# A two-layer decoder trunk: the last layer serves its expert groups in numerical order

## The chip, the cores and the metric

The kernel runs on one core of one Trainium2 chip. The core has a TensorE (PE in the profile; its weight loads are listed apart as PEld), a VectorE (DVE), a ScalarE (ACT), a GpSimd (POOL) and a SyncE (SP). Here SP does little but issue the DMAs that bring the weights from HBM into on-chip memory; 16 DMA engines move them. The metric is the device time of one execution in microseconds (us), and a kernel's time is the median over its runs.

## What is computed

There are 256 tokens of width 1024 and two layers. Each layer has a token mixer of four attention kinds, a cross-attention into 256 memory tokens, and a mixture of experts. The change is in the last of these. Cut down, it is:

```python
g_idx = jnp.argmax(xs @ w_group + b_group, axis=-1)            # one of 8 groups for each token
e_logits = (xs @ w_expert + b_expert).reshape(s, 8, 4)[jnp.arange(s), g_idx]
top_val, top_idx = lax.top_k(e_logits, 2)                      # two of the group's 4 experts
top_w = jax.nn.softmax(top_val, axis=-1) * g_weight
gates = one_hot(g_idx[:, None] * 4 + top_idx, 32) . top_w
hid = jax.nn.silu(xs @ w_gate[e]) * (xs @ w_up[e])             # for each expert e, 1024 -> 256
ff = sum over e of (hid * gates[:, e]) @ w_down[e]             # 256 -> 1024
x = layer_norm(ALPHA * x + ff)
```

An expert has three weight matrices (gate, up, down), each 1 MB as the kernel loads it. A layer has 8 groups of 4 experts, so 96 such loads. How many tokens an expert has depends on the data.

## The kernel before

**A group's work.** `moe` runs over the groups in the order of the table `SERVED` (line 34), one call of `expert(g)` for each (lines 1404 to 1476). The four experts of a group are worked on side by side: each has 32 columns of the 128-wide tiles. One pass therefore takes up to 32 tokens of each expert. A group's first pass is: the gate product (`up_to`, L1277, 64 matmuls) and its silu (L1281, on ACT), the up product (again L1277) and the multiplication with the silu (L1284, on DVE), a gather of the next group's tokens by matmuls with a 0/1 matrix (L1227, with L460 and L462 behind it), two transposes of the hidden values (L1290), and the down product (`rows`, L1306, with L1310 and L1311 behind it), whose results go back to the tokens' places (`back`, L1322 and L1327).

**Further passes.** Where an expert has more than 32 tokens, `over` (L1368) takes branches for a second pass, beyond 64 for a third, and so on. They stand between the first pass's transposes and its down product. In a group that isn't in `SPREAD` each further pass is a `whole` one: gather, gate, up, down. In a group that is (group 0 of the last layer), the further passes first do only gather, gate and up (`part`), each keeping its hidden values in a tile of its own; then the gate and up weights are given back (`free(g, 0, 8)`), and only then come these passes' down products (`rest`), and the group's own.

**The weights' places.** All weights of a layer stand in one list, the plan, in the order in which they will be used; for the experts the plan follows `SERVED` too (line 233): for each group 4 gate, 4 up and 4 down matrices. In the last layer's expert stage the loads go into 21 slots of 1 MB: 6 named main, 7 named ext that belong to this stage, 2 more ext and the two halves of M, and R, VM, KT and xx, which the attention has no more use for. `feed` (L255 to L280) issues the plan's next load on SP as soon as a slot is free, and SP takes them strictly in that order. `free` and `done` give a slot back: the 8 of a group's gate and up matrices after the last pass that uses them, that is behind the branches of `over`, and the 4 of its down matrices after its own down product. SP takes part in the branches, so a load behind `over` waits until TensorE has come through them.

**Known and unknown counts.** The first 21 expert loads are issued (at L270) before the router has run, for every expert. Later ones are issued at L275 inside a branch (L274) on the expert's token count, and are left out where it is 0.

**Hints.** `foresee` places a branch hint for TensorE ahead of a branch. `TELL` says at which of the eight steps of the up product the one for a group's second pass stands: in the last layer after step 3, and for the group that is served first after all eight, since its count is read only then. The group that is served first also does `prepare` (L1243 to L1255) between its gate and up products. `FIRST` and `GNUM` follow from `SERVED`: they say which number a group has in the code by which tokens are found.

Of the kernel before, what the change touches and what calls it, by code (L numbers as in the profile page):

```python
# [30 lines left out]
KEYS = 4  # L31


SERVED = [(0, 1, 2, 3, 4, 5, 6, 7), (1, 3, 0, 2, 4, 5, 6, 7)]
SPREAD = [(), (0,)]
TELL = [(3, 6), (3, 8)]


FIRST = [o[0] for o in SERVED]
GNUM = [[f if g == 0 else 0 if g == f else g for g in range(8)] for f in FIRST]  # L40
# [130 lines left out]
def trunk(ctx, tc, a, out, dbg=None, depth=DEPTH):  # L171
# [10 lines left out]
    def one(pool, name, shape, dt=F32):  # L182
        return tiles(pool, name, 1, shape, dt)[0]
# [27 lines left out]
    def square(l, m, q):  # L211
        wsq_i[l][m][q] = item(a["wsq"][l, m, q])
# [11 lines left out]
    for l in range(depth):  # L224
# [5 lines left out]
        for m in (3, 4):  # L230
            for q in range(4):
                square(l, m, q)
        for g, h in [(g, h) for g in SERVED[l + 1 == depth] for h in range(3)]:
            ids = exp_i[l].setdefault(g, {})
# [859 lines left out]
    def moe(l, pz, pb):  # L1094
# [3 lines left out]
        ff = one(pz, "ff", [128, 2, D])  # L1098
        served, spread = SERVED[late], SPREAD[late]
        follow = dict(zip(served, served[1:]))  # L1100
# [507 lines left out]
```

## Time and profile before

| What | Value |
|---|---|
| Time, median of 3 runs | 1009.5 us (1008.58 to 1012.58) |
| The profiled execution's own time | 1013.67 us |
| Its span, first to last instruction | 1011.9 us |
| TensorE matmul busy | 923.1 us, 91% |
| VectorE busy | 503.3 us, 50% |
| ScalarE busy | 340.9 us, 34% |
| Bytes moved by the DMAs | 272.59 MB, mean 269 GB/s |
| Stretch from 757 us to the end: DMA share, GB/s | 0.73, 295 |

The profile is of one execution. A row of the timeline gives start, duration, engine, line, operation and operands of one instruction or of several that are merged; in square brackets stands how long the engine was idle before it and what ended that. A row of the windows gives, for a stretch of time, each engine's busy us and instruction count, then TensorE's granted clock, the mean busy share of the 16 DMA engines, and what they moved in GB/s. Rows of the waits give a waiting line and what it waited for, then the sum in us, the number of waits and the longest.

The last layer's expert stage begins at about 757 us. Its groups were served in the order 1, 3, 0, 2, 4, 5, 6, 7. Group 0 took three further passes, group 2 one, the others none.

### The profile page before, as it was taken

To read this page: it belongs to the slowest core of one execution; us is meant where nothing else is said; L and a number is where in the kernel's file an instruction comes from. 1 tells how busy PE (TensorE), PEld (TensorE's weight loads), DVE (VectorE), ACT (ScalarE), POOL (GpSimd) and SP (SyncE) were. 2 spreads that over 40 slices of the span, in tenths; PEclk is the share of its full clock that TensorE was granted. 3 is DMA by queue.
4 is the path that set the end of the run, shared out by engine and by line. 5 is a ranking of instruction groups with operands and counts; after the bars stand their busy time and mean duration, and the time that the engine had idled before them with its cause. 6 is when DMAs were issued, how large, how long until landed. Compare 5 with 4: busy or idle time off the path is not lost. (4 is left out here: it accounts for less than half of the span.)

```text
span 1011.9 us, 19936 instructions
## 1 busy us (share of the span) xinstructions
PE 923.1 (91%) x7948; PEld 688.2 (68%) x7948; DVE 503.3 (50%) x1258; ACT 340.9 (34%) x736; POOL 0.2 (0%) x4
## 2 busy tenths in 40 slices
PE   7899999999998688989899999999999888997885
PEld 7888987898754354856368899789885564444541
DVE  5755755544653333323466575554465414644434
ACT  5454855343411121011144475435442121121111
POOL 0000000000000000000000000000000000000000
PEclk9999999999999899999999999999999999999998
DMA  9842334538769988999786244553784994719995
GB/s 351 343 147 99 134 128 161 209 125 331 293 268 422 424 348 367 424 425 420 250 336 229 108 147 180 174 208 110 288 351 196 421 387 183 318 58 421 422 363 203
DMA packets 43774, 272.59 MB, mean 269 GB/s; under 512 B 4832, under 2 KB 5344, under 8 KB 13280
## 3 DMA queue, kind: packets, MB, share of 16 engines
q1 hardware_dynamic: 43472, 270.26, 68.2%
q8 instruction: 86, 1.41, 0.5%
q14 instruction: 72, 0.59, 0.2%
q10 hardware_dynamic: 144, 0.33, 0.1%
HBM read 269.52 MB, written 1.05 MB: 267 GB/s over the span
## 5 line engine op out<-in xcount | busy, mean ns | idle before, releaser
L432 DVE SCALAR_TENSOR_TENSOR wl<-main,wh 128x1024 fp32r<-128x1024 f32 (+1 forms) x93 | 112.2, 1211 | 112.1 <-ACT wh L431 111.9
L431 ACT ACTIVATE wh<-main 128x1024 fp32r<-128x1024 f32 (+1 forms) x93 | 97.3, 1052 | 116.5 <-PE bank L438 68.3
L437 PE MATMUL bank<-xh,wh 128*128 128x256 f32 x368 | 108.8, 298 | 5.6 <-ACT xh L488 3.6
L438 PE MATMUL bank<-xl,wh 128*128 128x256 f32 x368 | 105.8, 288 | 1.0 <-DVE xl L432 0.6
L439 PE MATMUL bank<-xh,wl 128*128 128x256 f32 x368 | 104.9, 286 | 0.0
L1277 PE MATMUL bank<-ext,xg 128*32 128x256 f32 x912 | 88.2, 392 | 2.9 <-DMA ext<-exp 2.8
L1327 DVE TENSOR_TENSOR ff<-ff,bank 128x512 f32<-128x512 f32 x84 | 53.2, 681 | 49.9 <-PE bank L1322 49.9
L437 PEld LDWEIGHTS bank<-xh,wh 128*128 128x128 f32 x368 | 71.1, 194 | 7.0 <-ACT xh L488 4.1
L438 PEld LDWEIGHTS bank<-xl,wh 128*128 128x128 f32 x368 | 71.3, 194 | 2.2 <-DVE xl L432 0.9
L439 PEld LDWEIGHTS bank<-xh,wl 128*128 128x128 f32 x368 | 71.4, 194 | 0.1
L1277 PE MATMUL bank<-main,xg 128*32 128x256 f32 x640 | 66.1, 384 | 2.4 <-DMA main<-exp 2.4
L460 ACT ACTIVATE xg<-bank,prmb 128x128 f32<-128x128 f32 x64 | 24.0, 456 | 123.3 <-PE bank L1227 117.2
L1310 ACT ACTIVATE y<-bank,sm 128x512 fp32r<-128x512 f32 (+1 forms) x46 | 30.7, 669 | 103.5 <-PE bank L1306 76.1
L1322 PE MATMUL bank<-y,dt 128*128 128x512 f32 (+1 forms) x184 | 56.9, 422 | 7.9 <-DVE y L1311 7.2
L1306 PE MATMUL bank<-ext,dn 128*32 128x512 f32 (+1 forms) x212 | 46.6, 670 | 17.5 <-PEq L1368 6.8
L437 PE MATMUL bank<-wh,oh 128*128 128x512 f32 (+1 forms) x160 | 60.9, 380 | 0.0
L439 PE MATMUL bank<-wh,ol 128*128 128x512 f32 (+1 forms) x160 | 59.1, 369 | 0.0
L1322 PEld LDWEIGHTS bank<-y,dt 128*128 128x128 f32 x184 | 29.6, 188 | 43.2 <-ACT y L1310 16.4
L438 PE MATMUL bank<-wl,oh 128*128 128x512 f32 (+1 forms) x160 | 59.0, 369 | 0.0
L1277 PEld LDWEIGHTS bank<-ext,xg 128*32 128x32 f32 x912 | 42.6, 112 | 22.5 <-issue 4.7
L1227 PEld LDWEIGHTS bank<-dn,xhat 128*128 128x128 f32 x448 | 51.1, 192 | 5.8 <-issue 4.9
L1227 PE MATMUL bank<-dn,xhat 128*128 128x128 f32 x448 | 53.7, 278 | 0.0
(300 smaller groups left out, 2008.7 us busy)
## 6 DMA issues: line engine op xcount, KB each, us to landing
ext<-exp SPq DMA_DIRECT2D x75, 1024.0 KB, 16.6
main<-exp SPq DMA_DIRECT2D x54, 1024.0 KB, 12.8
main<-wsq SPq DMA_DIRECT2D x33, 1024.0 KB, 5.0
main<-win SPq DMA_DIRECT2D x22, 1024.0 KB, 6.8
M<-exp SPq DMA_DIRECT2D x17, 1024.0 KB, 15.0
VM<-exp SPq DMA_DIRECT2D x8, 1024.0 KB, 17.1
xx<-exp SPq DMA_DIRECT2D x7, 1024.0 KB, 14.0
M<-wsq SPq DMA_DIRECT2D x5, 1024.0 KB, 7.1
```

The costliest lines, as they stand in the source:

```text
L431: ACT.activation(hi, src, AF.Copy, scale=scale)
L432: DVE.scalar_tensor_tensor(lo, src, scale, hi.bitcast(F32), op0=ALU.mult, op1=ALU.subtract)
L437: PE.matmul(psum, lh, rh, start=first, stop=False, skip_group_check=True)
L438: PE.matmul(psum, lh, rl, start=False, stop=False, skip_group_check=True)
L439: PE.matmul(psum, ll, rh, start=False, stop=last, skip_group_check=True)
L460: ACT.activation(dst, src, AF.Identity, bias=b, scale=g)
L1227: PE.matmul(b[:, k * 128:(k + 1) * 128], xhat[:, t, c:c + 128], d[:, t], start=(t == 0 and k == 0), stop=(t == 1), skip_group_check=True)
L1277: PE.matmul(pg[m * i:m * i + m, which * S:(which + 1) * S], x[:, k, m * i:m * i + m], w[:, k], start=(k == 0), stop=(k == 7), skip_group_c ...
L1306: PE.matmul(b[m * i:m * i + m], ht[:, f * 128 + m * i:f * 128 + m * i + m], w[:, o:o + n], start=(f == 0), stop=(f == 1), skip_group_check ...
L1310: ACT.activation(hi, b, AF.Copy, scale=gate)
L1322: PE.matmul(bs[t], dt[:, t * 128:(t + 1) * 128], y[i], start=(i == 0 and not held), stop=(i == 1), skip_group_check=bool(held))
L1327: DVE.tensor_add(o, o, bs[t])
```

## The change

```diff
-SERVED = [(0, 1, 2, 3, 4, 5, 6, 7), (1, 3, 0, 2, 4, 5, 6, 7)]
+SERVED = [(0, 1, 2, 3, 4, 5, 6, 7), (0, 1, 2, 3, 4, 5, 6, 7)]
 SPREAD = [(), (0,)]
 TELL = [(3, 6), (3, 8)]
```

The last layer serves its groups as 0, 1, 2, 3, 4 and so on. Four things follow from the one row: the plan has the experts' loads in this order, so that the 21 loads ahead of the stage are group 0's twelve and nine of group 1's (before: group 1's twelve and nine of group 3's); `expert` is called in this order; group 0 is the one that does `prepare` and has its hint after all eight steps; and `GNUM` is the numbers 0 to 7. From group 4 on nothing changes its place. The first layer is as it was.

On ScalarE, right behind the first served group's branch, the further passes were whole ones: xx is the gathered tokens, hs the silu, f the transposed hidden values, y the down product. Before:

```order
L460 ACTIVATE xx_0_69<-bank_5_66,prmb_0_73 128x128 x4
L1281 ACTIVATE hs_1_13923<-bank_4_65 128x256
L427 ACTIVATE f_61_1_13926<-bank_6_67 128x256
L1310 ACTIVATE y_0_13929<-bank_0_61,sm_18_96 128x512
L1310 ACTIVATE y_0_13931<-bank_1_62,sm_18_96 128x512
L1368 COMPARE_AND_BRANCH
```

and now, at the same place:

```order
L460 ACTIVATE xx_0_69<-bank_5_66,prmb_0_73 128x128 x4
L1281 ACTIVATE prmb_0_73<-bank_4_65 128x256
L1368 COMPARE_AND_BRANCH
L460 ACTIVATE xx_0_69<-bank_0_61,prmb_0_73 128x128 x4
L1281 ACTIVATE prma_0_72<-bank_1_62 128x256
L1368 COMPARE_AND_BRANCH
```

Group 0's passes, which keep their hidden values in prmb and prma, have come to the place where group 1's branches stood.

On SP, behind the first eight loads that the first served group's gate and up slots let in (the last of them is ext_0), there stood before the reading of the experts' counts, and then the loads into that group's four down slots:

```order
L275 DMA ext_0_13708<-exp 128x2048
L274 UNCONDITIONAL_BRANCH x2
L1205 TENSOR_LOAD used_0_118
L1205 ISA x2
L1205 TENSOR_LOAD used_0_118
```

and now:

```order
L275 DMA ext_0_13708<-exp 128x2048
L274 UNCONDITIONAL_BRANCH x2
L1368 COMPARE_AND_BRANCH x3
L1368 UNCONDITIONAL_BRANCH x4
L1205 TENSOR_LOAD used_0_118
```

The three branches of group 0's late down products (`rest`) now stand between the first eight loads and the next four.

## The prediction

> **What bounds the kernel now.** I read the chain of work that ended last first, since only what lies on it can move the end, then the windows of the last layer's expert stage, then who released the loads there. The chain's last 100 us, in order of time:
>
> ```profile
> 912.46 20.29 DMA main<-exp
> ...
> 932.82 20.55 DMA R<-exp
> ...
> 953.43 6.60 DMA ext<-exp
> ...
> 961.16 9.61 DMA main<-exp
> ...
> 970.85 7.49 DMA main<-exp
> ...
> 978.40 7.40 DMA ext<-exp
> ...
> 985.96 6.99 DMA VM<-exp
> ...
> 992.99 1.90 PE bank L1306 x10
> ```
>
> From 912.5 us to 993 us the end hangs on expert weights arriving, one behind the other; TensorE, 91% busy over the span, only takes them up. After that come some 19 us of last products, layer norm and stores, which the change doesn't touch. So the question is when the loads of this stage run, and when they stand still. The windows, cut where the loads start and stop (columns as in the table above: the last two are DMA share and GB/s):
>
> ```profile
> 759.00:773.00 14.00, 12.29 (x166) 8.28 (x162) 8.94 (x41) 3.35 (x10) 0.00 (x0) 1.00 0.10 20
> 773.00:835.00 62.00, 55.32 (x716) 35.23 (x708) 21.44 (x64) 10.74 (x26) 0.00 (x0) 1.00 0.97 405
> 835.00:850.00 15.00, 12.17 (x170) 8.09 (x174) 4.21 (x17) 2.27 (x6) 0.00 (x0) 1.00 0.09 22
> 850.00:872.00 22.00, 20.80 (x152) 7.82 (x144) 16.09 (x42) 5.58 (x9) 0.00 (x0) 1.00 0.88 370
> ...
> 887.00:908.00 21.00, 18.81 (x218) 10.09 (x221) 7.27 (x20) 4.79 (x12) 0.00 (x0) 1.00 0.08 20
> 908.00:958.00 50.00, 41.78 (x456) 22.69 (x452) 23.33 (x73) 8.45 (x18) 0.00 (x0) 0.97 1.01 419
> ```
>
> The loads stand still three times (20 to 22 GB/s), while TensorE works, and run at full rate between. From 908 us on they don't stop again. What ends the standstills is told by SP's waits from 757 us on and by its issues:
>
> ```profile
> SPq L275 <- PEq L1368: 66.4, 4, 30.6
> ...
> SPq L275 <- PE bank L1306: 19.7, 4, 18.8
> ```
>
> ```profile
> 771.09 1.08 SPq L275 DMA_DIRECT2D main<-exp  x2
> 847.68 0.33 SPq L275 DMA_DIRECT2D main<-exp  x1
> 872.48 0.33 SPq L275 DMA_DIRECT2D VM<-exp  x1
> 905.55 0.33 SPq L275 DMA_DIRECT2D ext<-exp  x1
> 927.51 0.33 SPq L275 DMA_DIRECT2D M<-exp  x1
> ```
>
> SP waits for TensorE to come through a group's branches (L1368), that is for the 8 gate and up slots, and for a group's down products (L1306), that is for the 4 down slots. The issues are: 771.09, group 1's gate and up slots; 847.68, group 0's, after its three further passes; 872.48, group 0's down slots; 905.55, group 2's gate and up slots, after its further pass; 927.51, group 4's. The standstill that ends at 905.55 us is the last. **What sets the end is when TensorE comes through group 2, and how many loads are left then.** Both move.
>
> **How many loads are left.** In the stretch from 760 to 905 us the queue moved:
>
> ```profile
> q1 hardware_dynamic: 5184, 37.75, 63.3%
> ```
>
> At 1 MB (1.0486 million bytes) each these are 36 loads, as many as the slots of groups 1, 3 and 0 (12 each). With the 21 that were there before, 57 of the plan's expert loads are in when group 2's gate and up slots come free. With the new order only groups 0 and 1 are done before group 2: 24 slots, 45 loads. **12 loads more are left at that point**: the last three of group 3 and the first nine of group 4. All twelve moved bytes in the row above, so none of them is one that would be left out. A load's price comes from the full-rate stretches:
>
> ```profile
> 776.00:834.00 58.00, 51.86 (x687) 34.14 (x689) 18.63 (x53) 9.66 (x25) 0.00 (x0) 1.00 0.99 413
> 911.00:956.00 45.00, 37.03 (x406) 20.71 (x404) 18.40 (x55) 7.07 (x16) 0.00 (x0) 0.96 1.01 422
> ```
>
> At 422 GB/s a load takes 2.485 us, at 413 it takes 2.54. The first is from the stretch that is prolonged, so I take it: 12 x 2.485 = 29.8 us later; at most 30.5.
>
> The row's 422 GB/s also weighs a rule of the Trainium skill, "DMA: Bandwidth & Descriptors", section "Where 436 GB/s comes from": for transfers from HBM the memory's share of about 358 GB/s for a core is the limit. By it a load would take 2.93 us, the twelve 35.1 us (an estimate from that page), and the sum below would be 5.3 us higher. The trace disagrees, at 422 GB/s over 45 us, so the sum stays with the row.
>
> **When TensorE comes through group 2.** The silu of a group's first pass (L1281) marks each group's beginning. On ScalarE:
>
> ```profile
> 761.54 0.38 ACT L1281 ACTIVATE hs<-bank 128x256 f32<-128x256 f32 x1 [2.12 <-PE bank L1277]
> 780.19 0.38 ACT L1281 ACTIVATE hs<-bank 128x256 f32<-128x256 f32 x1 [3.89 <-PE bank L1277]
> 801.25 0.38 ACT L1281 ACTIVATE hs<-bank 128x256 f32<-128x256 f32 x1 [6.25 <-PE bank L1277]
> 877.89 0.38 ACT L1281 ACTIVATE hs<-bank 128x256 f32<-128x256 f32 x1 [4.54 <-PE bank L1277]
> ```
>
> These are groups 1, 3, 0 and 2. Group 1 took 18.65 us to the next group's silu, group 3 took 21.06, group 0 took 76.64. With the new order group 0 comes first, group 1 second, and group 2 third: group 3's turn is no longer ahead of group 2. If group 1 in second place takes as long as group 3 did there, the gain is 18.65 us; if it keeps its own time, 21.06. The first is nearer, because the 2.4 us between them belong to the place: the first group's end is quick because nothing of an earlier group is in its way. I take 19.0 us, with 18.65 and 21.06 as bounds.
>
> What comes on top is a wait of TensorE. Group 0's first further pass begins with a gather by a matrix that VectorE makes (L1219). As the third group it had that matrix early. As the first it gets it at the place where group 1's branch had its own made, here with TensorE's transposes (L1290) and gather ahead of them:
>
> ```profile
> 757.81 3.66 PE L1277 MATMUL bank<-main,xg 128*32 128x256 f32 x64
> ...
> 766.01 3.84 PE L1227 MATMUL bank<-dn,xhat 128*128 128x128 f32 x32
> 769.68 0.38 PE L1290 MATMUL bank<-cst,hs 128*128 128x128 f32 x2
> ...
> 770.49 0.35 DVE L1219 SCALAR_TENSOR_TENSOR f<-cst,sm,f 128x128 f32<-128x128 f32 x1
> ```
>
> The transposes end at 770.06 and the matrix at 770.84, so the gather starts 0.8 us late. The waits of TensorE and VectorE from 757 us on bound it:
>
> ```profile
> PE bank L1227 <- DVE f L1219: 2.9, 2, 1.5
> ...
> DVE dt L1266 <- DVEq L1368: 16.2, 6, 5.5
> ```
>
> TensorE waited for such a matrix twice, up to 1.5 us. I take 0.8, between nothing and 1.5. The hint is later too, after all eight steps of the up product instead of three. That takes five eighths of 3.66 us, 2.3 us, off its lead, and leaves the 3.84 us of gather and the transposes between hint and branch. I cost it at nothing, hidden by these. If they don't suffice, the second row bounds it: VectorE waited up to 5.5 us behind a branch.
>
> **What is hidden.** Group 0's three further passes and its late down products move as they are; they are in the 76.64 us. Its gate and up slots came free 46.4 us after its silu (801.25 to 847.68), so now at 761.5 + 46.4 + 0.8, about 809 us, and its down slots 71.2 us after it (872.48), about 834 us. The first standstill, which ended at 771, lasts until 809. That costs nothing by itself, as long as TensorE doesn't run out of weights. From SP's loads at L275, the time from issue to landing:
>
> ```profile
> DMA to landing us min/median/max: 4.8/13.2/21.5
> ```
>
> A first load takes 4.8 us, each further one 2.5. Group 1's gate and up matrices and one of its down matrices are among the first 21 loads. The eight issued from 809 us are its other down matrices, group 2's gate and one up matrix, in by 831; group 1's down product comes after its branch, 9.55 us after its silu (761.54 to 771.09 before), and that silu is at 761.5 + 76.6 + 0.8 = 839. Group 2's other up matrices wait for group 0's down slots and are in by 846; its gate product begins 3.7 us ahead of its silu at 859.7 (877.89 - 19.0 + 0.8), at 856. Its last three down matrices wait for group 1's branch at 848.5 and are in by 858; they are used behind the branch. Group 3's gate and up matrices follow, in by 879, and its turn begins at about 892. The tightest margin is 10 us.
>
> After the last standstill group 2's 12 slots let in 12 loads, 29.8 us. Before, group 4's gate and up slots came free 22.0 us after group 2's (905.55 to 927.51). Group 3 is in that place now and has its weights, so the loads go on without a gap, with 7.8 us to spare. From group 4 on everything is as before, only later.
>
> **Sum.** 29.8 - 19.0 + 0.8 = **11.6 us later**. The profiled execution took 1013.67 us, and would take 1025.3. It stood 4.2 us above the median of the runs shown, 1009.5, so the same step from there gives **1021.1**.
>
> **Rivals.** In each the price is in us against before.
>
> *Worse than that.* The branch into group 0's passes is now taken before its code is there, and TensorE stands still for what VectorE's row shows, 5.5 us: +17.1, 1026.6 us. For it speaks the later hint, against it that the queue is empty then (20 GB/s from 759 to 773 us), so that code would come fast. The Trainium skill's page "Runtime: NRT & Kernel Launch", section "Instruction fetch mechanics", says that a branch to code outside the two pages held must first fetch it; by that rule the stall could come here, and no run here shows it for TensorE with this hint. The trace agrees for VectorE, with the 5.5 us.
>
> *No change.* TensorE's work sets the end, and the same work in another order ends at the same time: 1009.5 us. For it speaks TensorE's 91%; against it the chain, in which loads stand for nearly all of 912 to 993 us, and the last full-rate stretch, where TensorE is busy for 37.0 of 45 us.
>
> *Faster.* Loads are issued without a look at the counts only ahead of the router. Before, these were group 1's twelve and nine of group 3's; after, group 3's are all behind the counts, and any expert of it without tokens is left out, three loads each. This gives a gain once over 4.7 loads (11.6 / 2.485) are saved behind the last standstill, two experts' worth: 11.6 - 14.9 = -3.3, 1006.2 us. Against it: three of group 3's experts had their down loads issued behind the counts in the trace, so at most one is empty, and what it saves lies ahead of the standstill, where loads wait for TensorE anyway.
>
> **Chances.** 0.76 for the forecast, 0.11 for worse, 0.08 for no change, 0.05 for faster. The forecast's bounds are 29.8 - 21.06 + 0 = +8.7 and 30.5 - 18.65 + 1.5 = +13.4, so 1018.2 to 1022.9. The three runs shown lie 4 us apart; half of that on either side makes 1016 to 1025. To hold 8 in 10 this isn't enough at 0.76, so the range reaches up over the worse case and down to where no change ends, 1014 to 1028, and leaves out the two others. About 0.5%, 5 us, can be told from no change: faster 0.05, the same 0.09 (no change, and a forecast that comes out at under half its size), slower 0.86.
>
> **What would show it.** In the changed kernel's profile: one standstill from 759 to about 809 us, and the last one ending at about 887 us (905.55 - 19.0 + 0.8 = 887.4) instead of 905.55; group 0's silu to group 1's in about 77 us; from 887 us on loads at some 420 GB/s without a stop until group 7's smaller pieces; a chain that again ends in loads. It would be wrong if TensorE waited for weights ahead of group 2 (the margin of 10 us is worked out, not seen), if the loads stopped again after 887 us, or if the branch into group 0's passes cost microseconds.

## The result, and the profile after

| | Before | Change |
|---|---|---|
| Time, median (range, runs) | 1009.2 us (1008.6 to 1012.6, 4) | 1021.3 us (1018.3 to 1026.0, 4) |
| Ratio, 95% interval | | 1.0117 (1.007 to 1.0164) |
| Time of the profiled execution | 1013.67 us | 1022.49 us |
| Its span | 1011.9 us | 1020.7 us |
| First silu of the stage (group 1 before, group 0 now) | 761.54 us | 757.26 us |
| From there to the end of the span | 250.4 us | 263.4 us |

The change costs 12.1 us, 1.2%. The two profiled executions lie only 8.8 us apart, since the stage began 4.3 us earlier in the second, though the program ahead of it is the same. Other executions began it at 753 to 764 us, so it is compared from its first silu on. A profile of one experiment, the change without SPREAD, fell into a disturbed execution of 1041 us; its three other runs took 1025 to 1031, and only they are in its median and ratio.

The windows of the profile after, cut where the loads of the last layer's expert stage stand and run (busy time of each engine, then granted clock, DMA share and GB/s):

```profile
757.00:804.00 47.00, 42.02 (x590) 29.44 (x586) 14.12 (x48) 8.61 (x23) 0.00 (x0) 1.00 0.01 2
804.00:829.00 25.00, 22.72 (x160) 8.62 (x160) 18.48 (x53) 6.14 (x11) 0.00 (x0) 1.00 0.74 296
830.00:843.00 13.00, 12.70 (x168) 8.45 (x166) 5.68 (x13) 0.86 (x3) 0.00 (x0) 1.00 0.76 316
843.00:880.00 37.00, 34.00 (x404) 20.05 (x404) 14.60 (x42) 8.50 (x20) 0.00 (x0) 1.00 0.85 343
886.00:918.00 32.00, 29.20 (x344) 16.58 (x345) 14.99 (x41) 3.93 (x9) 0.00 (x0) 0.95 1.01 420
918.00:956.00 38.00, 27.30 (x238) 14.80 (x240) 10.90 (x31) 5.33 (x13) 0.00 (x0) 0.91 1.01 424
956.00:1005.00 49.00, 40.66 (x387) 18.54 (x380) 16.12 (x46) 7.55 (x14) 0.00 (x0) 0.90 0.95 357
```

One standstill (2 GB/s) of 47 us while TensorE does group 0's four gate and up products, then loads in shorter runs up to 880, and from 886 us on full rate. SP's issues in the same profile's timeline, the first after each group's release:

```profile
803.83 0.34 SPq L275 DMA_DIRECT2D main<-exp  x1
...
828.65 0.34 SPq L275 DMA_DIRECT2D ext<-exp  x1
...
842.82 0.34 SPq L275 DMA_DIRECT2D KT<-exp  x1
...
880.42 0.33 SPq L275 DMA_DIRECT2D main<-exp  x1
...
902.05 0.33 SPq L275 DMA_DIRECT2D ext<-exp  x1
```

These are group 0's gate and up slots, its down slots, and the gate and up slots of groups 1, 2 and 3. The last release after which the loads had stood still is group 2's, at 880.42 instead of 905.55 us. ScalarE's timeline, the first silu of groups 0, 1, 2 and 3:

```profile
757.26 0.39 ACT L1281 ACTIVATE hs<-bank 128x256 f32<-128x256 f32 x1 [2.11 <-PE bank L1277]
...
834.06 0.39 ACT L1281 ACTIVATE hs<-bank 128x256 f32<-128x256 f32 x1 [4.54 <-PE bank L1277]
852.78 0.39 ACT L1281 ACTIVATE hs<-bank 128x256 f32<-128x256 f32 x1 [3.90 <-PE bank L1277]
893.09 0.39 ACT L1281 ACTIVATE hs<-bank 128x256 f32<-128x256 f32 x1 [7.75 <-PE bank L1277]
```

Group 0 took 76.8 us to group 1's silu, and group 1 took 18.7. The chain that ended last starts in this profile only with group 7's down product:

```profile
998.67 5.03 PE bank L1306 x16
1003.70 1.91 PE bank L1345 x4
```

The chain names no load any more, but its first piece holds waits for them: 16 matmuls that take 1.9 us where the weights are there (in a kernel shown below) took 5.03. The trace's landings agree: the last 1 MB matrices, in pieces, landed up to 1004.74 us, and the chain's matmuls take them up one by one (a piece of R landed at 999.12 and was used at 999.2, one of VM landed at 1000.46 and was used at 1000.5). From there on it is no longer waiting that makes the piece long. TensorE's granted clock was 0.50 from 999.7 to 1003.1 us, and its matmuls took up to 1.06 us instead of 0.59 (durations in ns, shortest, median and longest):

```profile
L1306 PE MATMUL bank<-VM,dn x4: 637/1061/1063, 1000.5 to 1003.1; 128*32 128x512 f32 x4
```

**Where the 13.1 us of the stage come from**, each difference between the two traces:

| Stretch | Before | After | Difference |
|---|---|---|---|
| First silu to group 2's release | 144.01 | 123.16 | -20.85 |
| Release to the first landing behind it | 5.68 | 5.18 | -0.50 |
| The twelve further loads, landing to landing (885.60 to 918.26) | | 32.66 | +32.66 |
| All later landings, to the last | 86.50 | 86.48 | -0.02 |
| Last landing to the end of the span | 14.17 | 15.96 | +1.79 |

The row before the last is the clearest finding here: once the same number of loads is left, the two kernels take the same time for 86 us. That they agree to 0.02 us is in part luck: other profiles shown below give 85.7 to 86.6 us for it. The last row isn't the change's: a second profile of the change, whose clock was full at this place, has 14.03 us in it. With the half clock TensorE took 6.0 us from its first use of VM to its last down products (1000.50 to 1006.47), in the profile of before 4.7 us (992.99 to 997.66).

### The profile page after: what moved, and what is told of

It is laid out like the page before. It is cut to its first block, busy times and chain, and to the rows that moved or that the text cites. A ratio compares the mean times of both kernels' runs of the same rounds, so it can differ in the third digit from the quotient of the medians.

```text
span 1020.7 us, 19935 instructions
## 1 busy us (share of the span) xinstructions
PE 926.6 (91%) x7948; PEld 685.9 (67%) x7948; DVE 504.3 (49%) x1258; ACT 341.3 (33%) x736; POOL 0.2 (0%) x4
## 2 busy tenths in 40 slices
DMA packets 43629, 271.52 MB, mean 266 GB/s; under 512 B 4816, under 2 KB 5328, under 8 KB 13264
## 5 line engine op out<-in xcount | busy, mean ns | idle before, releaser
L1277 PE MATMUL bank<-main,xg 128*32 128x256 f32 x640 | 70.1, 418 | 8.3 <-DMA main<-exp 4.7
L1306 PE MATMUL bank<-ext,dn 128*32 128x512 f32 (+1 forms) x212 | 46.2, 641 | 14.3 <-DMA main<-exp 5.9
L1277 PEld LDWEIGHTS bank<-main,xg 128*32 128x32 f32 x640 | 32.9, 119 | 31.8 <-issue 7.6
## 6 DMA issues: line engine op xcount, KB each, us to landing
VM<-exp SPq DMA_DIRECT2D x8, 1024.0 KB, 18.2
```

The costliest lines, as they stand in the source:

```text
L1277: PE.matmul(pg[m * i:m * i + m, which * S:(which + 1) * S], x[:, k, m * i:m * i + m], w[:, k], start=(k == 0), stop=(k == 7), skip_group_c ...
L1306: PE.matmul(b[m * i:m * i + m], ht[:, f * 128 + m * i:f * 128 + m * i + m], w[:, o:o + n], start=(f == 0), stop=(f == 1), skip_group_check ...
```

## The experiments

The theory is that of the prediction: the end is the time at which TensorE comes through group 2, the last standstill, plus the loads then left. The rivals were that group 0's place at the front (its long standstill, its branches) makes the kernel slower, that the bytes moved are what counts, and that TensorE's work is the bound. All ratios are to runs of the kernel before on the same chip: median 1008.8 us (18 runs) beside the first four kernels, 1010.0 (29 runs) beside the next four, one run (1008.1 us) beside the last two. The diffs of the orders show only the end of the row `SERVED`, the last layer's entry, twice against the change and twice against the kernel before.

### Group 0 first, but group 3 still ahead of group 2

```diff
-(0, 1, 2, 3, 4, 5, 6, 7)]
+(0, 1, 3, 2, 4, 5, 6, 7)]
```

> Order 0, 1, 3, 2, 4, 5, 6, 7: group 0 is first, as in the change, but group 3 stands ahead of group 2 again. My theory (the time is set by when TensorE comes through group 2 and how many loads are left then): three groups are done ahead of group 2, so 57 loads are in, and TensorE has done the same work by then as in the kernel before; group 2's branches are through at about the same distance from the stage's start, and the time is that of before, 1008 to 1013 us (ratio 0.999 to 1.004). Rival (group 0 in first place is what costs, by the long standstill of the loads at the start or by its late hint): about 1020 us, as the change (ratio 1.01).

Measured: 1012.8 us (12 runs), ratio 1.0044 (1.0021 to 1.0067). Group 0 is first as in the change, and some 8 of the change's 12 us are gone. So its place at the front isn't what costs; what group stands ahead of group 2 is. About 4 us stay, and the timeline shows a place for them. TensorE behind group 2's branches in this kernel, and SP's release there:

```profile
896.77 2.46 PE L1322 MATMUL bank<-y,dt 128*128 128x512 f32 x8
904.63 3.78 PE L1306 MATMUL bank<-main,dn 128*32 128x512 f32 x20 [5.40 <-PEq L1368]
```

```profile
904.19 1.07 SPq L275 DMA_DIRECT2D ext<-exp  x2
```

In the profile of before the same place reads:

```profile
902.97 2.46 PE L1322 MATMUL bank<-y,dt 128*128 128x512 f32 x8
905.97 3.59 PE L1306 MATMUL bank<-main,dn 128*32 128x512 f32 x29 [0.54 <-PEq L1368]
```

TensorE stood 5.4 us behind the branches (0.54 before), and group 2's release came 149.4 us after the first silu (904.19 - 754.8) instead of 144.0. The release sets the end, so these 5 us go straight into it; the stage of this profile is 4.4 us longer than that of before (254.8 against 250.4).

### Group 0 second, the rest in numerical order

```diff
-(0, 1, 2, 3, 4, 5, 6, 7)]
+(1, 0, 2, 3, 4, 5, 6, 7)]
```

> Order 1, 0, 2, 3, 4, 5, 6, 7: group 0 isn't first any more, and group 2 is still ahead of group 3. My theory: two groups are done ahead of group 2, 45 loads are in, 12 more are left than before, and TensorE is there some 19 to 21 us earlier: +9 to +13 us, 1018 to 1023 us (ratio 1.009 to 1.013). Rival (group 0 in first place is what costs): near before, 1008 to 1012 us.

Measured: 1022.7 us (6 runs), ratio 1.0136 (1.0102 to 1.017). Group 1 is first as before, its slots come free early, and the kernel is as slow as the change. Group 2's release in this kernel is SP's issue

```profile
880.60 0.33 SPq L275 DMA_DIRECT2D main<-exp  x1
```

123.9 us after the first silu (756.7), as in the change (123.2). This and the run above are the change's two halves: between this run and the change, the place of group 0 against group 1 costs nothing that can be seen; between the run above and the change, group 3's move behind group 2 costs some 8 us. The 4 us that the run above has over before aren't of either kind; they are of the size of its stand behind the branches.

### One group more ahead of group 2

```diff
-(1, 3, 0, 2, 4, 5, 6, 7)]
+(1, 3, 0, 4, 2, 5, 6, 7)]
```

> Order 1, 3, 0, 4, 2, 5, 6, 7: the kernel before with groups 2 and 4 exchanged, so that group 2's further pass comes one light group later. My theory, turned round: four groups are done ahead of group 2, 12 loads fewer than before are left (-30 us), TensorE comes through group 2 some 20 us later, so -8 to -10 us if loads then still set the end; TensorE's own work from there (groups 5, 6, 7) may bound it first, then -5 to -8 us: 1000 to 1004 us (ratio 0.991 to 0.996). If instead TensorE's work alone sets the end, no change from before: 1009 us.

Measured: 1003.2 us (7 runs), ratio 0.9924 (0.989 to 0.9959). **It beats both kernels**, the one before by 0.8% and the change by some 2%. The release is late, after another 18.8 us of TensorE's work (926.78, with the first silu at 764.0, is 162.8 us on, against 144.0), and twelve loads fewer are left:

```profile
926.78 0.33 SPq L275 DMA_DIRECT2D M<-exp  x1
```

At 2.7 us a load this gives 18.8 - 32.4 = -13.6 by the loads alone; measured in the stage are -12.0 (238.4 against 250.4), and -5.6 between the medians. The stages are of one execution each, so the medians count; what makes the rest of the difference stays open. The chain that ended last in this kernel, to set beside that of after:

```profile
983.44 1.92 PE bank L1306 x16
985.37 1.91 PE bank L1345 x4
```

The same 16 matmuls take 1.92 us, at full clock, instead of 5.03. Among TensorE's waits from 757 us on one alone is put down to a load, 0.5 us at 805 us, long before the end; the longest sums are

```profile
PE bank L1306 <- ACTq L1368: 8.3, 5, 1.7
PE bank L1322 <- DVE y L1311: 3.9, 5, 1.2
```

### Two groups more ahead of group 2

```diff
-(1, 3, 0, 2, 4, 5, 6, 7)]
+(1, 3, 0, 4, 5, 2, 6, 7)]
```

> Order 1, 3, 0, 4, 5, 2, 6, 7: group 2 one more place later than in the order that was faster than before. Theory: with group 4 ahead of group 2 the loads have stopped setting the end already (there the chain ended in TensorE's, VectorE's and ScalarE's work), so a further step brings nothing: 1001 to 1005 us, ratio 0.992 to 0.997. Rival (each light group put ahead of group 2 saves some 6 us): 997 us.

Measured: 1007.7 us (12 runs), ratio 0.9975 (0.995 to 1.0001). **Missed**: with TensorE as the bound one step further should have changed nothing, and it was 4.4 us slower than the step before (5.1 us by the ratios, whose intervals just touch). TensorE's timeline at group 5's down product, now ahead of group 2:

```profile
904.40 0.38 PE L1290 MATMUL bank<-cst,hs 128*128 128x128 f32 x2
908.78 3.64 PE L1306 MATMUL bank<-ext,dn 128*32 128x512 f32 x16 [3.99 <-DMA main<-exp]
```

The profile puts these 3.99 us down to a load, but by the plan group 5's last down matrices are the three behind the first 57, which landed by 896.3 us, and no load landed at 908.8 (the nearest at 906.99 and 909.49). It is again a stand behind branches; one of 3.1 us ahead of group 7's down product comes on top. In the waits from 757 us on, all stands of this kind sum to 14.3 us here (6.7 put down to ScalarE's branches, 3.6 to TensorE's, and the 4.0) and to 10.0 us in the order before this one (8.3 and 1.7). Where TensorE is the bound, these 4.3 us agree with the 4.4 us that were lost. So this run doesn't tell against the theory, but it doesn't test it finely either.

### The change without SPREAD

```diff
-SPREAD = [(), (0,)]
+SPREAD = [(), ()]
```

> The change's order with no group spread: group 0's further passes are whole ones, so its gate and up slots come free only about when its down slots do, some 24 us later, and the first standstill of the loads lasts 24 us longer, until about 827 us. My theory: the first standstill costs nothing by itself as long as the 23 loads that were let in before group 2's release are done by then; they now end at about 887 us, some 4 us behind the release, and TensorE may wait 1 or 2 us for group 2's up matrices: +1 to +6 us against the change, 1022 to 1027 us. Rival (every us that the loads stand still is a us of the time): +20 us or more, 1041 us.

Group 0's further passes are whole ones here, and its gate and up slots come free only after all of them. Measured: 1029.3 us (3 runs), ratio 1.018 (1.0142 to 1.0217). SP's first issue after the first standstill:

```profile
840.55 0.34 SPq L275 DMA_DIRECT2D main<-exp  x1
```

The first standstill ended 76.9 us after the first silu instead of 46.6 in the change, 30.3 us later, while the time rose by only some 6 to 8 us between the medians. The length of the first standstill isn't the price; the rival's 1041 us is 10 us and more above the three runs. The forecast was still too low by 2 us. I had not counted that whole passes may cost TensorE itself more. In this profile group 0 took 87.4 us against 76.8, and group 2's release came 135.8 us after the first silu against 123.2; but in the 87.4 us the clock was at half for 10.2 us, which by itself can make up to 5 us, and TensorE stood 3.3 us behind a branch, so what whole passes cost by themselves isn't shown.

### The change again, and with one group's loads left out

The change a second time, then with group 3's twelve weight loads of the last layer left out, then with group 4's. In both, the groups work on what the slots hold. The edit in `feed`, for group 3 (for group 4: 16 and 20):

```diff
-                if n is None:
+                l_, e_ = uses.get(i, (0, 0))
+                if l_ == 1 and 12 <= e_ < 16:
+                    pass
+                elif n is None:
```

> The change itself once more, as the reference for the two kernels with loads left out. Theory and rival: 1021 us, ratio 1.012 to before.

> The change with group 3's 12 weight loads left out in the last layer (its products are then of what lies in the slots; TensorE's work is the same). Theory: of these loads nine lie ahead of group 2's release, where the loads stand still and wait for slots anyway; only the three behind it save time, 3 x 2.5 us: 7 to 8 us below the change, 1012 to 1015 us. Rival (the bytes of the stage set its time, wherever they lie): 12 x 2.5 us = 30 us below the change, down to what TensorE alone needs, about 999 us.

> The change with group 4's 12 weight loads left out instead, as many bytes. Theory: all 12 lie behind group 2's release, so the loads end 30 us earlier and TensorE's own work from there sets the end: groups 3 to 7 at 20 us each put group 7's silu at about 973 us instead of 990.7 in the profile, so 18 to 22 us below the change, 999 to 1004 us. Rival (the place of the bytes doesn't matter): the same as with group 3's loads left out.

| Kernel | Time (runs) | Ratio | Against the change again |
|---|---|---|---|
| The change again | 1022.8 us (4) | 1.0146 (1.0106 to 1.0187) | |
| Without group 3's loads | 1012.5 us (10) | 1.0043 (1.0016 to 1.0069) | -10.3 us |
| Without group 4's loads | 1006.3 us (10) | 0.9972 (0.9946 to 0.9999) | -16.5 us |

Both leave out the same 12.6 MB. A skipped load keeps its place in the plan and its slot, so at group 2's release nine of group 3's twelve are already past, and three are saved behind it; of group 4's, all twelve are. If only bytes counted, both would gain about the same, some 30 us. They differ, in the order of the theory; the intervals of the two gains, some 5 us either way, hold the forecast 7 to 8 for group 3 and a part of the 18 to 22 for group 4, whose 1006.3 us lies 2 us above the range that was forecast. There TensorE becomes the bound, and it stood behind branches again (`L1371` is L1368, three lines on in this kernel). Its longest sum of waits from 880 us on:

```profile
PE bank L1309 <- PEq L1371: 10.6, 3, 3.9
```

The change's second profile also repeats the accounting: release 123.2 us after the first silu, the twelve further landings in 31.9 us, and the later ones in 86.6. With 14.0 us behind the last landing its stage is 261.0 us, 10.7 above that of before.

### Are the waits behind the branches chance?

Two of the kernels above, each in a second execution: the orders 0, 1, 3, 2 and 1, 3, 0, 4, 5, 2.

> Order 0, 1, 3, 2, 4, 5, 6, 7 once more, for one profile. In the first one TensorE stood 5.4 us behind group 2's branches, ahead of its own down product (899.2 to 904.6 us), which group 2 of the kernel before didn't (0.5 us). If this belongs to where the code lies in the program, it stands at the same place again with 5 to 6 us; if it comes from what else is going on in that execution, it is gone or elsewhere.

> Order 1, 3, 0, 4, 5, 2, 6, 7 once more, for one profile. In the first one TensorE stood 4.0 us between group 5's transposes and its down product, where the order 1, 3, 0, 4, 2, 5, 6, 7 stood 1.65 us, and 3.1 us ahead of group 7's down product. If it belongs to the code's place, the same two again; if not, gone or elsewhere.

Measured: 1014.1 us and 1009.5 us. In the order 0, 1, 3, 2 TensorE stood again behind group 2's branches, 5.85 us. The sum over its two waits, in the first and the second execution of that kernel:

```profile
PE bank L1306 <- PEq L1368: 9.9, 2, 5.4
```

```profile
PE bank L1306 <- PEq L1368: 9.9, 2, 5.8
```

In the order 1, 3, 0, 4, 5, 2, the first execution's 3.99 us at group 5 were 4.25 us in the second, now put down to the branches, and group 7's 3.1 us were 3.75:

```profile
904.60 2.33 PE L1306 MATMUL bank<-ext,dn 128*32 128x512 f32 x12 [4.25 <-PEq L1368]
```

So the stands of over 3 us belong to the program, not to the execution. What in the program makes them wasn't tried.

## Why the prediction was right

The forecast was 1021.1 us, and the median is 1021.3. The mechanism stood; two of its terms were off by more than the sum shows.

- **TensorE comes through group 2 earlier: forecast -19.0, with the first gather -18.2; measured -20.85.** Of the bounds 18.65 and 21.06 I took the lower, arguing that the 2.4 us between groups 1 and 3 belong to the place and not to the group. That was wrong: group 1 in second place kept its own 18.7 us, so the whole 21.06 of group 3 was gained.
- **The first gather: forecast +0.8 (0 to 1.5); measured none.** TensorE's timeline after:

```profile
765.40 0.38 PE L1290 MATMUL bank<-cst,hs 128*128 128x128 f32 x2
766.12 1.13 PE L1227 MATMUL bank<-f,xhat 128*128 128x128 f32 x8 [0.33 <-ACT xg L460]
```

The gather starts 0.34 us after the transposes, and its wait is for ScalarE's copy, not for VectorE's matrix. This also answers the rival "worse": the branch into group 0's passes didn't make TensorE stand, with the later hint. Since the same kernel family shows stands of 3 to 6 us at other branches, this was less safe than the chance of 0.11 made it look.
- **Twelve loads: forecast 29.8, at most 30.5; measured 32.7, outside the bound.** The change's second profile has 31.9, the order 1, 0, 2, 3 has 31.2, so the bound is passed each time. This is the mis-sized term. I priced a load by the bytes of the full-rate stretch, 2.485 us at 422 GB/s. What TensorE waits for is landings, and they come more slowly. In the profile of before, the queue between the landings of 911.23 and 956.81 us moved

```profile
q1 hardware_dynamic: 2620, 19.08, 100.1%
```

19.08 MB is 18.2 loads, while 17 landed: 45.58 / 17 = 2.68 us. A load is whole when its last piece is there, and at the later landing more of the following loads had already been moved than at the first. The price from landings, 12 x 2.68 = 32.2, stood in the profile of before and would have been within 0.5 us of what came. The rule of the Trainium skill ("DMA: Bandwidth & Descriptors", "Where 436 GB/s comes from") that I weighed gave 35.1; the trace after disagrees with its 358 GB/s as before, at 420 and 424 GB/s in the windows above.
- **The rest unchanged: forecast 0; measured +1.3** (-0.50, -0.02 and +1.79 of the table). The +1.79 goes for the most part with the half clock of that one execution, as said below the table; the second profile's three terms sum to -0.4.
- **Cover.** The first standstill ended 46.6 us after group 0's silu (forecast 47.2), group 0 took 76.8 us (76.6 + 0.8), group 3's release came 21.6 us after group 2's (22.0). TensorE waited for no weights ahead of group 2: its waits from 757 to 882 us hold no row with a load. From 886 us on the loads didn't stop. One sign came only in part: the chain doesn't end in loads by name; its matmuls wait for pieces up to 1000.46 us, and behind that the clock has its share.
- **Rivals.** "No change" falls: TensorE's work is the same, and the end came 12 us later. TensorE becomes the bound one step further on, in the order 1, 3, 0, 4, 2, where it waits for no load behind 805 us. "Faster" falls too: one load fewer was moved (271.52 MB against 272.59), a down matrix of group 1, and it lay ahead of the last standstill, where it saves nothing.

So +2.9 for the loads, -1.85 for the turn that is gained, -0.8 for the gather and +1.3 for the ends make 13.1 us out of 11.6 in the stage. In the second profile of the change the same stage rose by 10.7. That the median rose by 12.1 and the profiled execution by 8.8 is the spread between executions; the forecast's hit to 0.2 us is luck within some 3 us.

## What to carry to other kernels

Where weights stream through a limited set of slots, look for the last point at which the stream stands still, and count the loads that are left there: the end is that time plus these loads, and work that has its weights is moved ahead of that point until TensorE, not the loads, is the bound. Here one further group ahead of it was better than the order before, and a second gained nothing more. Price a load by the distance of landings over a long stretch, not by bytes per second.

## What the runs showed of the hardware

- **TensorE stands 3 to 6 us behind branches, at places that depend on the program.** In the change the longest such stand from 757 us on was 1.7 us in both profiles; in the order 0, 1, 3, 2 it was 5.4 and 5.8. The kernel before has one too, ahead of group 4's down product, where the loads hide it:

```profile
927.69 4.46 PE L1306 MATMUL bank<-ext,dn 128*32 128x512 f32 x20 [4.15 <-DMA main<-exp]
```

The load it is put down to isn't group 4's: its last three down matrices are the first three loads behind group 2's release, in by 916.10 us. Serving groups in another order moves the branches in the code, so a change of order has a price of some us that the order itself doesn't tell. The traces show one thing more. In the 5.4 us of the order 0, 1, 3, 2 (899.23 to 904.63) one packet of 16 KB ran on a queue that the trace calls instruction:

```profile
q8 instruction: 1, 0.02, 1.2%
```

It is the same in all fifteen stands of over 3 us ahead of a down product in these traces, and TensorE went on 1.5 to 2.1 us after that packet's end. In the 2 us before the end of the stands of 0.55 us no such packet ended. The Trainium skill ("Runtime: NRT & Kernel Launch", "Instruction fetch mechanics") says that a taken branch to code that isn't held must first fetch it; that would fit, but no run here separates it from another cause.
- **Executions of one kernel differ by 10 us and more, with the granted clock.** Runs of before beside the second set of kernels took 1004 to 1009 us at a mean clock of 0.984 to 0.987 and 1011 to 1018 at 0.974 to 0.976. Two profiles can't be subtracted as wholes; the stage has to be measured from a mark inside it. The clock differs inside the stage too (0.90 to 0.95 in the last three windows of the profile after, 0.97 in that of before from 908 to 958 us). While loads are the bound that costs little, as the 86.50 and 86.48 us show.
